# A list scheduler's costs: a sum that goes on in its PSUM tile, and four durations

## The chip, the cores and the metric

One core of a Trainium2 chip runs the whole program. The metric is device time in microseconds (us) of one execution, the median of three runs. The traces come from the hardware profiler and show one execution each.

## The reference, cut to what matters

Two decoder layers on x of shape (1, 512, 1024). Each layer normalizes x, projects it to 8776 columns with one weight matrix, and feeds three mixers whose outputs are gated, merged and multiplied with a last matrix:

```python
for l in range(DEPTH):                                  # DEPTH = 2
    h = rms_norm(x, norm_g[l])
    p = h @ w_in[l]
    (cb, cc, cx, cgate, q, k, v, agate, iq, ik, iw, pu, pgate, mgate) = split_columns(p)
    y_a = short_conv_mixer(cb, cc, cx, cgate, conv_w[l], w_out_conv[l])
    y_b = sparse_attention_mixer(q, k, v, agate, iq, ik, iw, ...)   # top 128 of up to 512 keys by an indexer's score
    y_c = pool_mixer(pu, pgate, pool_w[l], pool_scale[l], w_out_pool[l])
    g = jax.nn.sigmoid(mgate.reshape(B, S, N_BRANCHES, D))
    merged = g[:, :, 0] * y_a + g[:, :, 1] * y_b + g[:, :, 2] * y_c
    x = x + merged @ w_o[l]
```

## The kernel before, in words

Everything is kept transposed: 128 features on the partitions, the 512 positions along the free dimension. Every float32 operand of a matmul is split into a high and a low float32r part, and a product is the sum of three matmuls into one PSUM tile (`mm3`, line 393). A projection (`project`, line 456) takes one weight chunk of 128 x 1024 (`take`, line 375; `prep`, line 362, loads it, ACT makes the high part `whi` at line 371, DVE the low part `wlo` at line 372, three buffers of each) and adds up 8 x 3 matmuls of 512 columns in one of four PSUM tiles `pj`. DVE then reads the tile out (`evac`, line 385, or line 608, or line 819 at the end of a layer).

Beside the projections, TensorE computes scores in two tiles `sc`, and attention outputs in one tile `pv`, and transposes into one tile `pt`:

- `select` (line 556) makes the indexer's scores: per layer 24 pairs of matmuls of 256, 384 or 512 columns into an `sc` tile, each pair one sum (lines 563 and 564). Afterwards DVE finds the 128 largest of each row by 16 rounds of MAX8 and MATCH_REPLACE8 for each of three blocks of rows (lines 576 and 577).
- `attention` (line 712) runs twice in a layer over 16 blocks: a pair of matmuls of 128 to 512 columns into `sc` (lines 719 and 720), softmax on DVE and ACT (lines 724 to 730), one to four transposes into `pt` (line 738), which ACT and DVE split into a high and a low part (lines 741 and 742), and for each of 4 heads a sum of eight matmuls of 512, 512, 384, 384, 256, 256, 128 and 128 columns into `pv` (lines 748 to 753).

`merge` (line 591) multiplies a branch's output with its matrix, gates it, and adds it to the accumulators on GpSimd (line 610).

The order in which each engine issues is not the order of the code. The class `Order` (line 30) reads all instructions, gives each a cost (`cost`, line 108), and plays them through a model of the engines (`play`, line 139): whenever an engine is free, it takes that instruction among those ready that has the smallest priority number. For TensorE the number is the place in the program; for the others it is the time at which TensorE needs the result, worked out backwards from the pass before. An instruction is ready when what it depends on has ended, plus a latency from `LAT` or, for a reader on TensorE, from `TO_PE` (lines 37 and 38). Tiles with few buffers hold an instruction back until one is free. The play is repeated (`PASSES`, line 13), each time with new priorities, and the pass with the shortest modelled time is kept (`arrange`, line 247). It fixes each engine's order; on the chip an engine that reaches an instruction whose operands are not there waits, and all behind it with it.

With the latency of 0.003 from TensorE to TensorE, the next matmul of a sum is not yet ready at the moment at which the one before ends. So the play takes another sum's matmul, if one is ready, and two sums take turns in two PSUM tiles:

```python
LAT = {"PE": 0.2, "DVE": 0.13, "Activation": 0.14, "Pool": 0.1, "SP": 0.13}
TO_PE = {"PE": 0.003, "DVE": 0.255, "Activation": 0.27, "Pool": 0.2, "SP": 0.27}
    ...
ready[j] = max(ready[j], fin + self.lat(e, ops[j]["e"]))
```

Of the kernel before, what the change touches and what calls it, by code (L numbers as in the profile page):

```python
# [9 lines left out]
PSUM = bass.MemoryType.PSUM  # L10

LAG = 3
PASSES = 4
P = 128
S = 512
D = 1024
# [13 lines left out]
class Order:  # L30
# [4 lines left out]


    LAT = {"PE": 0.2, "DVE": 0.13, "Activation": 0.14, "Pool": 0.1, "SP": 0.13}
    TO_PE = {"PE": 0.003, "DVE": 0.255, "Activation": 0.27, "Pool": 0.2, "SP": 0.27}

    def lat(self, a, b):  # L40
        return self.TO_PE[a] if b == "PE" else self.LAT[a]

# [65 lines left out]
    def cost(self, inst, kind):  # L108

        def size(a):  # L110
            n = 1
            for _, k in a.bass_ap.ap[1:]:
                n *= k
            return n

        aps = [a for a in inst.ins if hasattr(a, "bass_ap")]
        out = inst.outs[0]
        n = size(out)
        psum = any(a.bass_ap.tensor.name.split("_")[0] in ("pj", "sc", "pt", "pv") for a in aps)
        wide = [a for a in aps if size(a) > 1]  # L120
        extra = len(aps) > len(wide)
        engine = str(inst.engine).split(".")[-1]
        if kind == "InstMatmult":
            f32 = str(aps[0].dtype).endswith("float32")
            c = (0.0004167 * n + 0.003) * ((4 if n > 128 else 2) if f32 else 1)
            return c, 0.0
        if kind == "InstDMACopy":
            b = n * out.bass_ap.ap[0][1] * 4
            return (0.65 if aps[0].bass_ap.tensor.name in self.slot else 0.48), b / 360e3
        if engine == "Activation":  # L130
            return 0.093 - 0.042 * psum + 0.000833 * n + 0.093 * extra, 0.0
        if engine == "Pool":
            return (0.1 if kind == "InstMemset" else 0.1 + 0.0022 * n), 0.0
        if kind in ("InstMax", "InstMatchReplace"):
            return 0.069 + 0.00104 * max(size(a) for a in aps), 0.0
        fast = kind == "InstTensorScalarPtr" and len(wide) == 1 and not psum
        return 0.069 + 0.00104 * n * (0.5 if fast else 1) + 0.061 * extra, 0.0

# [107 lines left out]

    def arrange(self, passes=PASSES):
        raw = self.read()
# [695 lines left out]
```

## Time and profile before

| | us |
|---|---|
| median of 3 runs (1078.87 to 1079.73) | 1079.21 |
| the profiled execution's own time | 1078.84 |
| its span, first to last instruction | 1077.1 |
| TensorE busy in it | 1065.4 |
| VectorE (DVE) busy | 799.2 |
| ScalarE (ACT) busy | 465.5 |
| GpSimd (POOL) busy | 97.2 |

The span lies inside the execution's own time; 1.7 us of that time lie around it. Matmuls are pipelined, so that the length of one in the trace (some 0.39 us for 512 columns) is longer than the distance from its start to the next one's start; the distance is what counts for the time. The granted TensorE clock of the span is 1.000 of full speed.

### The profile page before, as it was taken

The page shows a single profiled execution, that of the slowest core. Times are in us where ns is not written, and L with a number is a line of the kernel's source. Part 1 is how long each engine was busy: PE and PEld are TensorE (multiplying, and loading weights), DVE is VectorE, ACT ScalarE, POOL GpSimd, SP SyncE. Part 2 cuts the span into 40 slices and gives each one's busy share as a digit, 9 for nine tenths or more (in the row PEclk, how much of TensorE's full clock was granted, in tenths as well). Part 3 has the DMA queues.
Part 4 walks back from the last instruction along what each step waited for, and adds up shares of the span by engine and source line. Part 5 has one row for each costly group of instructions (what it writes and reads, how often), then busy time and mean ns, then how long its engine had stood idle before and what let it go on. Part 6 is the DMA issues. An engine that isn't in the chain of part 4 may idle for free.

```text
span 1077.1 us, 13444 instructions
## 1 busy us (share of the span) xinstructions
PE 1065.4 (99%) x4842; PEld 878.4 (82%) x4842; DVE 799.2 (74%) x1389; ACT 465.5 (43%) x747; POOL 97.2 (9%) x76
## 2 busy tenths in 40 slices
PE   7999999999999999999999999999999999999998
PEld 6888888888888888888888888888888878888886
DVE  6889999997558865455559899999876598744442
ACT  6355233485233673233334542235852347623320
POOL 4000000000000011221210000000000001132210
PEclk9999999999999999999999999999999999999999
DMA  6542322452234522234535322225423245122352
GB/s 226 153 140 78 99 98 94 133 152 72 82 102 130 160 75 78 98 98 164 169 117 153 115 86 98 98 79 166 128 79 98 79 144 149 61 98 98 98 195 78
DMA packets 44402, 124.39 MB, mean 115 GB/s; under 512 B 6960, under 2 KB 7472, under 8 KB 44336
## 3 DMA queue, kind: packets, MB, share of 16 engines
q1 hardware_dynamic: 44336, 123.53, 36.4%
q8 instruction: 38, 0.62, 0.2%
q14 instruction: 28, 0.23, 0.1%
HBM read 101.49 MB, written 4.19 MB: 98 GB/s over the span
## 4 chain that ended last, share of the span: by engine, by line
PE 96%; DVE 1%; DMA 1%; issue 0%; ACT 0%; SPq 0%; DVEq 0%; ACTq 0%
PE pj L388 87%; PE sc L388 4%; PE pv L388 3%; PE pt L391 2%; DMA b<-in_x 0%; DVE wlo L372 0%; DMA k<-h 0%; DVE w L488 0%; SPq L355 0%; DVE h L401 0%; ACT whi L371 0%; DVE w L649 0%; ACT xhi L403 0%; DVE w L435 0%; DVE w L436 0%
## 5 line engine op out<-in xcount | busy, mean ns | idle before, releaser
L388 PE MATMUL pj<-xhi,whi 128*128 128x512 f32 x1040 | 373.1, 393 | 6.5 <-ACT whi L371 6.5
L388 PE MATMUL pj<-xlo,whi 128*128 128x512 f32 x1040 | 372.8, 393 | 0.0
L388 PE MATMUL pj<-xhi,wlo 128*128 128x512 f32 x1040 | 372.4, 393 | 0.0
L371 ACT ACTIVATE whi<-raw 128x1024 fp32r<-128x1024 f32 (+2 forms) x185 | 191.5, 1036 | 385.6 <-PE pj L388 358.9
L372 DVE TENSOR_TENSOR wlo<-raw,whi 128x1024 fp32r<-128x1024 f32 (+2 forms) x185 | 228.5, 1239 | 15.5 <-ACT whi L371 14.8
L388 PEld LDWEIGHTS pj<-xhi,whi 128*128 128x128 f32 x1040 | 195.0, 188 | 46.7 <-ACT whi L371 6.7
L388 PEld LDWEIGHTS pj<-xhi,wlo 128*128 128x128 f32 x1040 | 195.7, 188 | 39.4 <-DVE wlo L372 0.5
L388 PEld LDWEIGHTS pj<-xlo,whi 128*128 128x128 f32 x1040 | 195.5, 188 | 39.4
L388 PE MATMUL pj<-b,whi 128*128 128x512 f32 x640 | 210.7, 390 | 0.0
L385 DVE TENSOR_TENSOR w<-pj,ss 128x512 f32<-128x512 f32 x104 | 70.8, 684 | 93.3 <-PE pj L388 93.0
L388 PEld LDWEIGHTS pj<-b,whi 128*128 128x128 f32 x640 | 120.0, 188 | 24.2
L388 PE MATMUL pj<-b,wlo 128*128 128x512 f32 x320 | 118.2, 391 | 0.0
L610 POOL TENSOR_TENSOR b<-b,w 128x512 f32<-128x512 f32 x32 | 60.6, 1899 | 264.5 <-DVE w L608 264.4
L388 PEld LDWEIGHTS pj<-b,wlo 128*128 128x128 f32 x320 | 60.1, 188 | 12.3
L576 DVE MAX8 m<-score 128x8 f32<-128x256 f32 (+2 forms) x96 | 53.2, 557 | 1.7
L577 DVE MATCH_REPLACE8 score<-m,score 128x384 f32<-128x384 f32 (+2 forms) x96 | 52.0, 542 | 0.0
L742 DVE TENSOR_TENSOR pth<-pt,pth 128x128 fp32r<-128x128 f32 (+1 forms) x64 | 31.1, 486 | 18.7 <-PE pv L388 9.4
L819 DVE TENSOR_TENSOR w<-pj,w 128x512 f32<-128x512 f32 x16 | 11.0, 690 | 44.4 <-PE pj L388 42.8
L727 ACT ACTIVATE a<-a,mn 128x128 f32<-128x128 f32 (+1 forms) x64 | 35.6, 557 | 15.5 <-DVE mn L724 14.9
L665 POOL TENSOR_TENSOR w<-w,w 128x512 f32<-128x512 f32 x8 | 11.9, 1492 | 325.4 <-ACT w L664 325.4
L388 PE MATMUL pv<-pth,b 128*128 128x512 f32 (+3 forms) x128 | 39.9, 316 | 0.0
L741 ACT ACTIVATE pth<-pt 128x128 fp32r<-128x128 f32 (+1 forms) x64 | 27.6, 432 | 27.4 <-PE pt L391 20.1
(119 smaller groups left out, 999.7 us busy)
## 6 DMA issues: line engine op xcount, KB each, us to landing
raw<-in_w SPq DMA_DIRECT2D x177, 512.0 KB, 3.3
b<-h SPq DMA_DIRECT2D x128, 64.0 KB, 2.2
k<-h SPq DMA_DIRECT2D x64, 128.0 KB, 3.2
b<-in_x SPq DMA_DIRECT2D x8, 256.0 KB, 4.8
w<-in_x SPq DMA_DIRECT2D x8, 256.0 KB, 5.5
xs<-w SPq DMA_DIRECT2D x8, 256.0 KB, 2.3
w<-xs SPq DMA_DIRECT2D x8, 256.0 KB, 3.9
out_x<-w SPq DMA_DIRECT2D x8, 256.0 KB, 2.0
```

The source lines that it names most:

```text
L371: act.activation(hi[:, p], raw[:, p], AF.Copy)
L372: dve.tensor_tensor(out=lo[:, p], in0=raw[:, p], in1=hi[:, p].bitcast(F32), op=ALU.subtract)
L385: dve.tensor_tensor(out=out, in0=ps, in1=by, op=ALU.mult)
L388: pe.matmul(ps, lhs, rhs, start=start, stop=stop)
L391: pe.transpose(out, src, ident if n == P else ident[64:64 + n, 64:64 + n])
L576: dve.max(m8, score)
L577: dve.match_replace(score, m8, score, -3.0e38)
L610: gp.tensor_tensor(out=a, in0=a, in1=g, op=ALU.add)
L665: gp.tensor_tensor(out=s0, in0=s0, in1=s1, op=ALU.add)
L727: act.activation(pr[:, :w], pr[:, :w], AF.Exp, bias=mn, scale=-1.0, accum_out=zs)
L741: act.activation(dh, pst[:, :b + 1, :], AF.Copy)
L742: dve.tensor_tensor(out=dl, in0=pst[:, :b + 1, :], in1=dh.bitcast(F32), op=ALU.subtract)
```

## The change

Six numbers of the scheduler change. No instruction is added or removed; only the order in which the engines issue can differ. The cost of a float32r matmul of n columns goes from 0.0004167 n + 0.003 to 0.000423 n + 0.01 (for 512 columns from 0.2163 to 0.2266), of a float32 transpose of 128 columns from 0.1127 to 0.1283, of a GpSimd operation on 512 elements from 1.226 to 1.636, of MATCH_REPLACE8 on 512 elements from 0.601 to 0.677. The latency between two matmuls goes to zero, and six passes are played in place of four.

```diff
-PASSES = 4
+PASSES = 6
...
-    TO_PE = {"PE": 0.003, "DVE": 0.255, "Activation": 0.27, "Pool": 0.2, "SP": 0.27}
+    TO_PE = {"PE": 0.0, "DVE": 0.255, "Activation": 0.27, "Pool": 0.2, "SP": 0.27}
...
-            c = (0.0004167 * n + 0.003) * ((4 if n > 128 else 2) if f32 else 1)
+            c = (0.000423 * n + 0.01) * ((4 if n > 128 else 2) if f32 else 1)
...
-            return (0.1 if kind == "InstMemset" else 0.1 + 0.0022 * n), 0.0
+            return (0.1 if kind == "InstMemset" else 0.1 + 0.003 * n), 0.0
         if kind in ("InstMax", "InstMatchReplace"):
-            return 0.069 + 0.00104 * max(size(a) for a in aps), 0.0
+            n = max(size(a) for a in aps)
+            return 0.069 + 0.00104 * n + 0.076 * (kind == "InstMatchReplace"), 0.0
```

## Rows read from the trace of the kernel before

**Rows 1.** The page: busy time of two engines, and the chain that ended last.

```profile
PE 1065.4 (99%) x4842; PEld 878.4 (82%) x4842; DVE 799.2 (74%) x1389; ACT 465.5 (43%) x747; POOL 97.2 (9%) x76
...
PE 96%; DVE 1%; DMA 1%; issue 0%; ACT 0%; SPq 0%; DVEq 0%; ACTq 0%
```

**Rows 2.** Waits of PE: who it waited for, us in total, times, longest us.

```profile
PE pj L388 <- ACT whi L371: 6.5, 1, 6.5
PE sc L388 <- DVE w L649: 0.6, 1, 0.6
PE sc L388 <- DVE w L401: 0.3, 1, 0.3
PE sc L388 <- DMA k<-h: 0.2, 1, 0.2
```

**Rows 3.** The chain that ended last, one piece: start us, us, what.

```profile
100.39 76.16 PE pj L388 x336
```

**Rows 4.** Timeline of PE inside that piece: start us, us, instruction.

```profile
101.13 0.39 PE L388 MATMUL pj<-xlo,whi 128*128 128x512 f32 x1
101.36 0.39 PE L388 MATMUL pj<-b,whi 128*128 128x512 f32 x1
101.58 0.39 PE L388 MATMUL pj<-xhi,wlo 128*128 128x512 f32 x1
```

**Rows 5.** Timeline of PE from 599.78 us, where one sum runs alone.

```profile
599.78 0.39 PE L388 MATMUL pj<-xhi,whi 128*128 128x512 f32 x1
600.01 0.39 PE L388 MATMUL pj<-xlo,whi 128*128 128x512 f32 x1
600.24 0.39 PE L388 MATMUL pj<-xhi,wlo 128*128 128x512 f32 x1
...
601.82 0.62 PE L388 MATMUL pj<-xhi,whi 128*128 128x512 f32 x2
```

**Rows 6.** Timeline of PE from 73.89 us: score pairs of `select`.

```profile
73.89 0.28 PE L388 MATMUL sc<-b,b 128*128 128x256 f32 x1
74.00 0.63 PE L388 MATMUL pj<-xhi,whi 128*128 128x512 f32 x2
74.47 0.28 PE L388 MATMUL sc<-b,b 128*128 128x256 f32 x1
74.58 0.40 PE L388 MATMUL pj<-xlo,whi 128*128 128x512 f32 x1
74.82 0.40 PE L388 MATMUL sc<-b,b 128*128 128x256 f32 x2
75.06 0.40 PE L388 MATMUL pj<-xhi,wlo 128*128 128x512 f32 x1
```

**Rows 7.** Timeline of PE from 235.46 us: the end of a sum in `pv`.

```profile
235.46 0.44 PE L388 MATMUL pj<-xhi,whi 128*128 128x512 f32 x1
235.74 0.22 PE L388 MATMUL pv<-pth,b 128*128 128x128 f32 x1
235.80 0.45 PE L388 MATMUL pj<-xlo,whi 128*128 128x512 f32 x1
```

**Rows 8.** Timeline of PE at its longest stop after the start.

```profile
604.37 0.40 PE L388 MATMUL pj<-xlo,whi 128*128 128x512 f32 x1
605.38 0.39 PE L388 MATMUL sc<-b,b 128*128 128x256 f32 x1 [0.61 <-DVE w L649]
```

**Rows 9.** Groups by line and shape: count, busy us, mean ns, idle before.

```profile
L372 DVE TENSOR_TENSOR wlo<-raw,whi 128x1024 fp32r<-128x1024 f32 x177 | 219.2, 1242 | 15.2 <-ACT whi L371 14.6
...
L610 POOL TENSOR_TENSOR b<-b,w 128x512 f32<-128x512 f32 x32 | 60.6, 1899 | 264.5 <-DVE w L608 264.4 <-POOL b L610 0.2
...
L577 DVE MATCH_REPLACE8 score<-m,score 128x512 f32<-128x512 f32 x32 | 21.6, 676 | 0.0
...
L742 DVE TENSOR_TENSOR pth<-pt,pth 128x512 fp32r<-128x512 f32 x16 | 11.0, 689 | 5.0 <-ACT pth L741 5.0
...
L741 ACT ACTIVATE pth<-pt 128x512 fp32r<-128x512 f32 x16 | 9.4, 590 | 6.8 <-PE pt L391 6.7
```

**Rows 10.** Windows: us, busy (x) of PE PEld DVE ACT POOL, clock, DMA share, GB/s.

```profile
100.00:180.00 80.00, 80.00 (x354) 66.25 (x353) 76.53 (x165) 25.11 (x29) 1.52 (x1) 1.00 0.30 99
180.00:220.00 40.00, 40.00 (x179) 32.78 (x178) 39.67 (x69) 18.63 (x27) 1.29 (x1) 1.00 0.49 138
```

**Rows 11.** Timeline at the end: the last read of PSUM.

```profile
1073.31 0.69 DVE L819 TENSOR_TENSOR w<-pj,w 128x512 f32<-128x512 f32 x1 [1.80 <-PE pj L388]
```

## The prediction

> **What bounds the kernel.** I read the page first. TensorE is busy 99% of the span and holds 96% of the chain that ended last; DVE is next with 74% [rows 1]. So I ask what TensorE does in the rest of the time, and whether its matmuls follow each other as closely as they can. The waits of TensorE answer the first: 6.5 us before the first matmul, and then three named waits that make 0.6 + 0.3 + 0.2 = 1.1 us [rows 2]. The chain's long piece answers the second: 336 matmuls in 76.16 us are 0.2267 us from one start to the next [rows 3]. A quiet stretch has nothing more to give, and the span from 6.5 us to the last read of PSUM at 1073.31 us [rows 11] is nearly all such stretches, plus the stretches of `select` and `attention`, in which short matmuls and transposes come in between.
>
> **What the change can reach.** It removes and adds no instruction, so the time can move in two ways only: by the price of a neighbourhood on TensorE (which matmul stands behind which), and by waits of TensorE that go or come because an order fits the chip's durations better or worse.
>
> **Part 1, the long sums.** Now two sums take turns: between the second and the third matmul of one product stands one of another sum [rows 4]. With the latency at zero the next matmul of a sum is ready when the one before it ends, has the smaller number, and is taken. What does a change of tile cost here? In the stretch with turns the distance is 0.2267 us [rows 3]; where one sum runs alone, nine distances from 599.78 to 601.82 make 2.04 us, or 0.2267 each [rows 5]. The same. Some 4,200 of the 4,842 matmuls are of this kind by the loops of the code, and I put them at **0 us**. The rows of the nine are rounded to 0.01 us, which leaves 0.001 us for each; if about half of the 4,200 take turns today, that is 2 us either way, and the range has to hold it.
>
> **Part 2, the score pairs.** There are 2 x 24 pairs in `select` and 4 x 16 in `attention`, 112 in all, 224 matmuls. Taking turns, an `sc` matmul of 256 columns and two long ones take 74.47 - 73.89 = 0.58 us, so the short one costs 0.58 - 0.453 = 0.127; the next one with one long matmul takes 74.82 - 74.47 = 0.35, so 0.123. Side by side, two of them behind a long one take 75.06 - 74.58 = 0.48, or 0.127 each [rows 6]. So standing side by side is worth nothing that these rows show; their rounding leaves 0.01 us for each matmul either way, 224 x 0.01 = 2.2 us. I take **0**, and keep -2.2 and +2.2 us.
>
> **Part 3, the sums in `pv`.** Sixteen sums of eight, 128 matmuls. Taking turns, a long matmul and one of 128 columns take 235.80 - 235.46 = 0.34 us, so the short one costs 0.115 [rows 7]. Before shows no two of 128 columns of one such sum side by side. From below: the columns alone, a quarter of 0.2267, are 0.057; with 32 such matmuls here and as many among the scores that is 64 x 0.058 = 3.7 us to gain. From above: the price of today and the rounding, +0.01 for each of 128, 1.3 us lost. The nearest row is that of the pair of 256 columns, whose price did not move, so I stay near today's price: **-0.5 us**.
>
> **Part 4, the durations.** The plan of before lets TensorE run at 0.2163 us for a long matmul, 4.6% faster than the chip does. The other engines were planned too fast as well: `wlo` at 0.069 + 0.00104 x 1024 = 1.134 us against 1.242, the read of transposed tiles at 0.601 against 0.689 on DVE and 0.478 against 0.590 on ACT, MATCH_REPLACE8 at 0.601 against 0.676, the GpSimd sum at 1.226 against 1.899 [rows 9]. So errors of the same sign partly cancelled. The change mends TensorE (0.2266), MATCH_REPLACE8 (0.677) and most of GpSimd (1.636), and leaves `wlo` and the reads as they are. GpSimd's 32 sums lie beside matmuls (its engine idles 264.5 us before them), so I put that edit at 0; if that cover went, 32 x 0.41 us of better foresight would be at stake. Two more passes can only find a plan that the model likes better. What is to be had is the waits: of the 1.1 us named and the stop at 604.37 us, where 1.01 us pass from one start to the next in place of 0.23 [rows 8], I take **-0.5 us**. All of them gone would be -1.1 us, with the unnamed rest of the stop -1.3; what new waits could cost stands with the second rival. The 6.5 us at the start hang on the first weights and stay; one ACT operation of 0.6 us moved past the first `whi` would be the bound either way. At the end nothing stands behind the last sum but one DVE read and its DMA, in either order.
>
> **The sum.** 0 + 0 - 0.5 - 0.5 = -1.0 us. Against the profiled execution's own time (1078.84, which is 1.7 above its span) that is 1077.8; the median of the runs shown is 0.37 us higher, so **1078.2 us**. A measurement of this kernel can tell some 0.2%, 2.2 us, from no change: the forecast counts as no change.
>
> **The rivals.**
>
> *Side by side is cheaper, and the waits go.* If every `sc` matmul gains the 0.01 us that the rounding hides (2.2 us), the `pv` sums 1.0 and the waits 1.1, the time is 1079.2 - 4.3 = 1074.9. For it: a sum done sooner frees `sc` and `pv` sooner, which the loops of `select` and `attention` wait for. Against: rows 6. Chance 0.22.
>
> *Short matmuls side by side overlap.* The whole 3.7 us of part 3 in place of 0.5 give 1078.2 - 3.2 = 1075.0. For it: 0.06 us pass from the `pv` matmul to the long one behind it, so the short one does not hold the next matmul for longer; against: the long one before it is held 0.28 us in place of 0.227 [rows 7], so the price is paid there. Chance 0.08. The Trainium skill (TensorE: Matmul & The Clock Gate, Back-to-back issue gap) gives some 81 ns for each matmul in a sustained stream of loads and matmuls of 128 columns; by it the 64 short ones would save an estimated 64 x 0.034 = 2.2 us, while the trace's own price, where each stands alone, is 115 ns, so the rule is open until two stand side by side.
>
> *Slower: the margin is gone.* The 4.6% by which TensorE was planned too fast put more matmuls into each gap than the plan said, and covered the other engines' too short costs. With TensorE right, ACT and DVE are 10 to 23% slower than planned (1.242 for 1.134, 0.590 for 0.478) before what waits on them. The place is the loop from transposes over the two reads of `pt` (one buffer) to the next transposes, 64 times, and the loop over the two `sc` tiles, 48 times in `select`. A loop of about 2 us loses 4.6% of cover, 0.1 us; if TensorE arrives early by that in all 112, 11 us are lost, in one of three 3.7 us. In one of three, the time is 1078.2 + 3.7 = 1081.9. It decides from the point at which DVE has no slack: it is busy 76.53 of 80 us and 39.67 of 40 us in the search for the largest scores [rows 10]. Against: TensorE is busy all of those stretches today, and the search itself is what the change plans better. Chance 0.17.
>
> *The change does not do what it says.* If a play with the old kind of turns remains the best, or the order differs where nothing waits, the time stays at 1079.2. Chance 0.08, inside no change.
>
> **How the numbers follow.** Forecast 0.45, rivals 0.22, 0.08, 0.17 and 0.08. Of the forecast's own chance some 0.06 falls below 1077.05, the bound of faster. So faster is 0.22 + 0.08 + 0.06 = 0.36, no change 0.39 + 0.08 = 0.47, slower 0.17. The range reaches down to the two faster rivals with a little room, 1074.5, and up to the lower part of the slower one, 1081.4. The likeliest case alone is 1077 to 1079.5.
>
> **What would show it.** In the changed kernel's timeline the two parts of a product should stand behind each other (`xhi,whi`, `xlo,whi`, `xhi,wlo`) at 0.227 us, score pairs should show as x2, and `pv` sums as runs of eight. A window of a long projection stretch should hold as many matmuls as before; if it holds more, part 1 is wrong. Two `pv` matmuls of 128 columns side by side give the missing price of part 3. In the waits of TensorE, more than 2 us behind the start, with ACT and DVE as those waited for, would be the slower rival; none at all the first.

## The result, and the profile after

The changed kernel takes 1087.20 us (median of 4 runs, 1085.29 to 1088.57) against 1079.04 (4 runs, 1078.71 to 1079.73) of the kernel before: a ratio of 1.0074, with an interval of 1.0056 to 1.0091. It is slower by 8.2 us, outside what the interval leaves for no change, and outside the predicted range.

The profiled execution took 1088.57 us, its span 1086.4. Its line numbers from 136 on are one higher than before. First the busy times and the chain that ended last on its page, beside [rows 1]:

```profile
PE 1069.9 (98%) x4842; PEld 874.5 (80%) x4842; DVE 804.6 (74%) x1389; ACT 460.2 (42%) x747; POOL 84.2 (8%) x76
...
PE 80%; DVE 9%; ACT 4%; DMA 3%; issue 3%; SPq 1%; ACTq 0%; DVEq 0%
```

TensorE still looks full (98%), but its share of the chain fell from 96 to 80%: the chain now leaves TensorE for DVE, ACT and DMAs in many places. Had I read the busy share alone, I should have seen nothing. The waits of TensorE (total us, times, longest us), beside [rows 2]:

```profile
PE pj L389 <- ACT whi L372: 5.8, 2, 5.1
PE sc L389 <- ACT h L401: 2.3, 2, 1.2
PE pj L389 <- DVE wlo L373: 0.9, 2, 0.5
PE sc L389 <- DMA k<-h: 0.6, 1, 0.6
PE pv L389 <- ACT pth L742: 0.5, 1, 0.5
PE sc L389 <- DVE w L402: 0.5, 1, 0.5
PE pt L392 <- DVE w L530: 0.4, 1, 0.4
PE pj L389 <- DVE w L487: 0.4, 1, 0.4
PE pt L392 <- DVE pth L743: 0.4, 2, 0.2
PE pj L389 <- DVE xlo L405: 0.3, 1, 0.3
```

The first line holds the start (5.1) and a new wait of 0.7; with the nine below it that is 7.0 us behind the start, in place of 1.1. From all start-to-start distances of the trace, counting what a distance holds beyond the usual pitch of its shape (its median) where that is over 0.12 us, I get 26 stops of together 12.4 us, in place of 10 of together 3.1. (The view counts the time in which TensorE stood idle, this list what the next start lost, so it is the longer; the 0.7 at the second weights are 1.18 in it. Left out of it, at the very start, until about 12 us before and 11 us after, are the distances of 0.427 us at which the long matmuls follow there: the lower level of the clock.) This sum, "stops" below, is 9.3 us more, of the 10.7 by which the time from the first matmul's start to the last one's grew (1066.4 to 1077.1). The first matmul came 1.4 us earlier, which gives part of it back.

Where it was lost shows in windows of TensorE alone (start:end, length, busy us with matmuls, granted clock, DMA share, GB/s), first of the kernel before, then of the one after:

```profile
6.50:100.00 93.50, 93.49 (x411) 1.00 0.47 147
100.00:220.00 120.00, 120.00 (x532) 1.00 0.36 112
540.00:640.00 100.00, 99.39 (x449) 1.00 0.38 117
640.00:760.00 120.00, 120.00 (x536) 1.00 0.38 120
```

```profile
6.50:100.00 93.50, 90.17 (x394) 1.00 0.45 145
100.00:220.00 120.00, 120.00 (x532) 1.00 0.38 115
540.00:640.00 100.00, 97.86 (x440) 1.00 0.36 112
640.00:760.00 120.00, 120.00 (x535) 1.00 0.38 119
```

Over the whole span the changed kernel is 43 matmuls behind at 1073 us, and 26 of them are lost at the heads of the two layers: 17 before 100 us and 9 from 540 to 640. The search for the largest scores, where DVE has no slack and where I had put the point from which the slower rival decides, loses none in the first layer (532 and 532) and one in the second. The granted clock is printed as 1.00, full speed, in all of them; only the first matmuls of the span, told above, follow at the lower level in both kernels. The head of a layer is where the projections feed short chains: TensorE to DVE or ACT, through an SP-issued move of 64 KB, into the next splits. The longest stop of the first layer after the start, in the timeline (TensorE, ACT, DVE, then SP's queue):

```profile
65.54 0.39 PE L389 MATMUL pj<-xlo,whi 128*128 128x512 f32 x1
66.94 0.50 PE L389 MATMUL sc<-h,whi 128*128 128x512 f32 x1 [1.01 <-ACT h L401]
...
66.26 0.63 ACT L401 ACTIVATE h<-w 128x512 fp32r<-128x512 f32 x1 [2.43 <-DMA b<-h]
...
66.92 0.69 DVE L402 TENSOR_TENSOR h<-w,h 128x512 fp32r<-128x512 f32 x1 [1.95 <-ACT h L401]
...
55.01 10.89 SPq L356 DMA_DIRECT2D b<-h  x15
```

From 65.54 to 66.94 are 1.40 us in place of 0.23. Read it backwards: the matmul wants `h`, ACT makes it at 66.26 after 2.43 us of waiting for a DMA that still reads the tile it must write into, and that DMA is one of 15 that SP issues in a row from 55.01 to 65.90. The plan has 0.65 us for each, and 14 of them follow at that in the mean; one takes 1.73 us to issue, and that one makes the row some 1.2 us late, about what TensorE loses (1.17). The kernel before has such a move at about the same time. The two moves, after and before, in SP's timeline:

```profile
57.53 1.73 SPq L356 DMA_DIRECT2D b<-h  x1
...
55.77 1.52 SPq L355 DMA_DIRECT2D b<-h  x1
```

Before, no stop of TensorE follows on it: the first matmul on `h` there starts at 69.70, 0.22 us behind its neighbour. In an engine with a fixed order all later matmuls, ready or not, stand behind one that waits. In the second layer the matmul on `h` starts 1.64 us behind its neighbour in place of 0.23; there the 16 moves keep the plan's pace, but begin late.

The neighbourhoods did change as foretold. Timeline of TensorE after: a sum that goes on in its tile, then pairs of `sc`, then a run of `pv`.

```profile
120.14 0.39 PE L389 MATMUL pj<-xlo,whi 128*128 128x512 f32 x1
120.36 0.39 PE L389 MATMUL pj<-xhi,wlo 128*128 128x512 f32 x1
120.59 0.39 PE L389 MATMUL pj<-xhi,whi 128*128 128x512 f32 x1
...
70.69 0.64 PE L389 MATMUL sc<-b,b 128*128 128x256 f32 x4
71.17 0.39 PE L389 MATMUL pj<-xlo,whi 128*128 128x512 f32 x1
...
260.51 1.15 PE L389 MATMUL pv<-pth,b 128*128 128x512 f32 x7
261.49 0.45 PE L389 MATMUL pj<-xhi,wlo 128*128 128x512 f32 x1
```

And one piece of its chain (start us, us, what), beside [rows 3]:

```profile
102.84 75.25 PE pj L389 x332
```

75.25 / 332 = 0.2267 us: the pitch of the long matmuls is that of before, to four digits. So the loss is not in the price of a long matmul; most of it (9.3 us of 10.7) is in stops.

### The profile page after: what moved, and what is told of

Same layout as the page of the kernel before. It is cut to its first block, busy times and chain, and to the rows that moved or that the text cites. A ratio compares the mean times of both kernels' runs of the same rounds, so it can differ in the third digit from the quotient of the medians.

```text
span 1086.4 us, 13426 instructions
## 1 busy us (share of the span) xinstructions
PE 1069.9 (98%) x4842; PEld 874.5 (80%) x4842; DVE 804.6 (74%) x1389; ACT 460.2 (42%) x747; POOL 84.2 (8%) x76
## 4 chain that ended last, share of the span: by engine, by line
PE 80%; DVE 9%; ACT 4%; DMA 3%; issue 3%; SPq 1%; ACTq 0%; DVEq 0%
PE pj L389 72%; PE sc L389 4%; PE pv L389 3%; DVE wlo L373 2%; PE pt L392 2%; DMA b<-h 1%; DMA raw<-in_w 1%; SPq L356 1%; ACT whi L372 1%; DVE h L402 1%; DVE w L489 1%; DVE w L487 1%; ACT a L728 0%; ACT xhi L404 0%; DVE w L491 0%
## 5 line engine op out<-in xcount | busy, mean ns | idle before, releaser
L389 PE MATMUL pj<-xhi,whi 128*128 128x512 f32 x1040 | 408.7, 393 | 6.2 <-ACT whi L372 5.8
L389 PE MATMUL pj<-xhi,wlo 128*128 128x512 f32 x1040 | 408.1, 393 | 0.9 <-DVE wlo L373 0.9
L389 PE MATMUL pj<-xlo,whi 128*128 128x512 f32 x1040 | 407.3, 392 | 0.3 <-DVE xlo L405 0.3
L373 DVE TENSOR_TENSOR wlo<-raw,whi 128x1024 fp32r<-128x1024 f32 (+2 forms) x185 | 238.2, 1290 | 28.7 <-ACT whi L372 27.9
L389 PE MATMUL pj<-b,whi 128*128 128x512 f32 x640 | 198.9, 390 | 0.0
L389 PE MATMUL pj<-b,wlo 128*128 128x512 f32 x320 | 125.0, 391 | 0.0
L611 POOL TENSOR_TENSOR b<-b,w 128x512 f32<-128x512 f32 x32 | 45.7, 1427 | 281.7 <-DVE w L609 281.7
L578 DVE MATCH_REPLACE8 score<-m,score 128x256 f32<-128x256 f32 (+2 forms) x96 | 52.0, 542 | 0.0
L609 DVE SCALAR_TENSOR_TENSOR w<-w,pj 128x512 f32<-128x512 f32 x32 | 21.9, 685 | 32.2 <-ACT b L404 16.8
L401 ACT ACTIVATE h<-w 128x512 fp32r<-128x512 f32 (+1 forms) x36 | 22.7, 630 | 51.8 <-DVE w L490 24.1
```

Of the source, the lines that this page charges most:

```text
L373: dve.tensor_tensor(out=lo[:, p], in0=raw[:, p], in1=hi[:, p].bitcast(F32), op=ALU.subtract)
L389: pe.matmul(ps, lhs, rhs, start=start, stop=stop)
L401: act.activation(hi, src, AF.Copy)
L578: dve.match_replace(score, m8, score, -3.0e38)
L609: dve.scalar_tensor_tensor(a if first else g, g, 1.0, py, op0=ALU.add, op1=ALU.mult)
L611: gp.tensor_tensor(out=a, in0=a, in1=g, op=ALU.add)
```

## The experiments

Every kernel below does the same work; only the orders differ. All were timed beside the kernel before, which had a median of 1079.0 to 1079.1 each time. Two theories lead. **Margin**: planning TensorE 4.6% too fast was a cover for all that the model leaves out (landing times, queues, buffers); at the true pace an operand is planned to arrive just in time, comes late, and TensorE stops. **Draw**: any edit of the costs deals another order, and orders scatter by some us, whatever the edit. **Turns** is the other half of the change: that sums no longer take turns.

### The halves apart

`e1`: the kernel before with the latency at zero. `e2`: the changed kernel with 0.003 again. `e3`: the changed kernel with the old matmul cost. `e4`: the changed kernel with 0.2 us more latency from every other engine to TensorE.

```diff
-    TO_PE = {"PE": 0.003, "DVE": 0.255, "Activation": 0.27, "Pool": 0.2, "SP": 0.27}
+    TO_PE = {"PE": 0.0, "DVE": 0.255, "Activation": 0.27, "Pool": 0.2, "SP": 0.27}     # e1; e2 the reverse
...
-            c = (0.000423 * n + 0.01) * ((4 if n > 128 else 2) if f32 else 1)
+            c = (0.0004167 * n + 0.003) * ((4 if n > 128 else 2) if f32 else 1)          # e3
...
+    TO_PE = {"PE": 0.0, "DVE": 0.455, "Activation": 0.47, "Pool": 0.4, "SP": 0.47}       # e4
```

> The kernel before with one edit: the latency from TensorE to TensorE is 0 in place of 0.003; all durations as before, so TensorE is still planned 4.6% too fast. Theory M (the margin went with the matmul's true duration): no loss, 1077 to 1081 us, waits of TensorE behind the start under 2.5 us. Theory T (two sums taking turns is itself what kept TensorE fed): as slow as the change, 1084 to 1090. Theory C (any new order is a draw, and the one of before was a lucky one): anywhere from 1077 to 1090.

> The changed kernel with the latency of 0.003 back, so that two sums take turns again; durations as changed. Theory M: still slow, 1083 to 1090, since TensorE is planned at its true pace. Theory T: back to 1077 to 1081. Theory C: anywhere from 1077 to 1090.

> The changed kernel with the matmul's old cost, 0.0004167 n + 0.003, so that TensorE is planned 4.6% too fast again; sums still go on in their tile. Theory M: back to 1077 to 1081. Theory T: still slow, 1084 to 1090. Theory C: anywhere.

> The changed kernel with 0.2 us more on each latency into TensorE (DVE 0.455, ACT 0.47, GpSimd 0.4, SP 0.47), so that a matmul is planned only when its operand is surely there; matmul cost true, sums go on in their tile. Theory M: the margin is back in another form, 1076 to 1082, waits of TensorE behind the start under 3 us. Theory T: no help, 1084 to 1090. Theory C: anywhere.

| kernel | us | ratio to before, interval | stops, us |
|---|---|---|---|
| e1, latency zero alone | 1082.86 | 1.0032 (1.0020 to 1.0044) | 5.7 |
| e2, after with turns | 1091.42 | 1.0113 (1.0097 to 1.0128) | 11.1 |
| e3, after with old matmul cost | 1080.71 | 1.0015 (1.0005 to 1.0024) | 6.1 |
| e4, after with wide latencies | 1086.85 | 1.0071 (1.0054 to 1.0088) | 10.4 |

The matmul cost carries most of it: taking it back alone (e3) gives back 6.5 of the 8.2 us. Bringing the turns back (e2) makes it worse by 4.2, so the turns half is not the cause. But e1, the turns half alone at the old pace, is 3.7 us slower than before, where margin had foreseen no loss: a draw, or the turns, or both. A wider latency in front of TensorE (e4) does not help, against what margin had foreseen (1076 to 1082): 0.2 us of fixed latency there is not the cover that went.

### The pace alone

The changed kernel with four other matmul costs, and the kernel before with one; 512 columns then take, as planned, 0.2215 (`e6`), 0.2368 (`e7`), 0.2105 (`e11`, and `e12` in the kernel before). The chip takes 0.2267. A fifth, `e5` (0.0004 n, 10% too fast, expected at 1076 to 1081), gives no time: its engines' orders deadlock.

```diff
-            c = (0.000423 * n + 0.01) * ((4 if n > 128 else 2) if f32 else 1)
+            c = (0.00042 * n + 0.0065) * ((4 if n > 128 else 2) if f32 else 1)           # e6
+            c = (0.000443 * n + 0.01) * ((4 if n > 128 else 2) if f32 else 1)            # e7
+            c = (0.00041 * n + 0.0006) * ((4 if n > 128 else 2) if f32 else 1)           # e11, e12
```

> The changed kernel with a matmul planned at 0.00042 n + 0.0065 (0.2215 us, 2.3% faster than the chip), half way between e3 and the change. Theory M: between them, 1082 to 1086. Theory C: no relation, 1077 to 1090.

> The changed kernel with a matmul planned at 0.000443 n + 0.01 (0.2368 us, 4.5% slower than the chip). Theory M: worse than the change, 1090 to 1098, with more stops of TensorE behind DVE and ACT. Theory C: no relation, 1077 to 1090.

> The changed kernel with a matmul planned at 0.00041 n + 0.0006 (0.2105 us, 7% faster than the chip). Theory M: the next point of the series 0.2368, 0.2266, 0.2215, 0.2163: no worse than 1080.7, 1077 to 1081; below it nothing is left to gain but single stops. Theory C: anywhere to 1090.

> The kernel before with the matmul planned at 0.00041 n + 0.0006 (7% too fast in place of 4.6%), all else as before, so sums take turns. Theory M: as fast as before or faster, 1075 to 1080. Theory C: 1077 to 1090.

| planned for 512 columns | kernel | us | ratio, interval | stops, us |
|---|---|---|---|---|
| 0.2105 (7% fast) | e11 | 1081.93 | 1.0023 (1.0013 to 1.0033) | 6.9 |
| 0.2105, with turns | e12 | 1088.11 | 1.0081 (1.0064 to 1.0099) | 10.9 |
| 0.2163 (4.6% fast) | e3 | 1080.71 | 1.0015 (1.0005 to 1.0024) | 6.1 |
| 0.2215 (2% fast) | e6 | 1083.35 | 1.0042 (1.0027 to 1.0056) | 6.1 |
| 0.2266 (true) | after | 1087.20 | 1.0074 (1.0056 to 1.0091) | 12.4 |
| 0.2368 (4.5% slow) | e7 | 1113.84 | 1.0323 (1.0307 to 1.0338) | 34.6 |

From 4.6% fast to 4.5% slow the time only rises, as the margin theory has it, though each row is one order, and the step from e3 to e6 (2.6 us, with stops alike) is no larger than the scatter between orders shown below. The price of 4.5% slow is more than margin had foreseen (1090 to 1098). Waits of TensorE in e7:

```profile
PE sc L389 <- ACT w L401: 6.7, 5, 2.2
PE pj L389 <- ACT whi L372: 5.6, 2, 5.1
PE sc L389 <- DVE mn L725: 4.4, 5, 2.0
PE sc L389 <- DMA k<-h: 2.8, 2, 1.5
```

The second line is the start. The others are of the kinds seen in the changed kernel (splits, the moved `k`, the small chains), and several times longer. A plan that thinks TensorE slow leaves the feeding work for later. Too much margin does not go on helping, which margin had not foreseen (e11 1077 to 1081, e12 1075 to 1080): e11 and e12 have a few long stops. Waits of TensorE in e12:

```profile
PE pj L388 <- DVE b L710: 2.4, 1, 2.4
PE pj L388 <- DVE w L486: 1.8, 1, 1.8
PE pt L391 <- DVE w L529: 1.3, 1, 1.3
```

In the first two TensorE stops for reads by DVE of tiles in PSUM that it wants to write again, in the third for an operand. These stops stand in the plan itself. Played again, the scheduler of e12 leaves TensorE idle for 2.79, 1.95 and 1.53 us in front of these three instructions, where the chip lost 2.55, 1.94 and 1.50; that of e11 plans 3.72 us in front of the one that loses 2.40. So at 7% the model itself can no longer feed its TensorE without stops. The changed kernel's plan has one stop of 0.64 us behind its start (0.58 on the chip); the other 22 that the chip shows behind 12 us are in no plan.

### Is it the number, or the draw?

Each cost was moved by a hair: the true one (`n1`: 0.0095, `n2`: 0.0105 in place of 0.01) and the old one, in the changed kernel (`n3`: 0.0025, `n4`: 0.0035 in place of 0.003).

> The changed kernel with a matmul planned 0.5 ns shorter (0.000423 n + 0.0095): another order, at the same pace. Theory M (the true pace is what costs): 1085 to 1090, as the change. Theory C (the order of the change was an unlucky draw): back towards 1080 to 1083.

> The changed kernel with a matmul planned 0.5 ns longer (0.000423 n + 0.0105). Theory M: 1085 to 1090. Theory C: back towards 1080 to 1083.

> The changed kernel with the old matmul cost less 0.5 ns (0.0004167 n + 0.0025), a neighbour of e3. Theory M: 1079 to 1083, as e3. Theory C: as far from e3 as the change is, up to 1088.

> The changed kernel with the old matmul cost plus 0.5 ns (0.0004167 n + 0.0035), the other neighbour of e3. Theory M: 1079 to 1083. Theory C: up to 1088.

| pace | kernels | us |
|---|---|---|
| true | after, n1, n2 | 1087.20, 1087.96, 1087.61 |
| 4.6% fast, no turns | e3, n3, n4 | 1080.71, 1075.95, 1077.23 |

The means are 1087.6 and 1078.0: 9.6 us lie between the paces, while the three orders of a pace scatter over 0.8 and 4.8 us. So the pace decides, and a draw is worth a few us at the old pace. All eight kernels at the old pace (before, e1, e3, n3, n4, and e10, n6 and n7 from further down) lie between 1075.95 and 1082.86, and the five at the true pace with the feeders' costs as changed (after, n1, n2, e2, e4) between 1086.85 and 1091.42. The row of moves shows the cover at work: in all eight of the first kind one move takes 1.09 to 1.97 us, and TensorE does not stop at the first matmul on `h`; in after, n1, n2 and e7 a move of 1.5 to 1.9 us stops it there for 1.17 to 1.33 us (e2 does not stop there, e4 for 0.26). `n3` (ratio 0.9972, interval 0.9960 to 0.9983) is faster than both kernels, by 3.1 us than before. Its chain and waits of TensorE:

```profile
PE 96%; issue 1%; ACT 1%; DVE 1%; DMA 0%; SPq 0%; DVEq 0%
...
PE pj L389 <- ACT whi L372: 6.4, 1, 6.4
PE sc L389 <- issue: 0.8, 2, 0.5
PE pj L389 <- DVE wlo L373: 0.7, 2, 0.4
```

TensorE again holds 96% of the chain, with 2.9 us of stops.

### Can the cover be put where it belongs?

If the margin is a ratio between TensorE and what feeds it, then the true matmul cost with slower planned feeders must do as well. `e8`: DVE and ACT costs times 1.048. `e9`: every DMA lands 1 us later. `n5`: both.

```diff
-            return 0.093 - 0.042 * psum + 0.000833 * n + 0.093 * extra, 0.0
+            return 1.048 * (0.093 - 0.042 * psum + 0.000833 * n + 0.093 * extra), 0.0    # e8, n5; the two DVE lines alike
...
-                        fin = dma + 0.78
+                        fin = dma + 1.78                                                 # e9, n5, n7
...
-                need[i] = (min(s) if s else t) - c - (x + 1.43 if x else 0)
+                need[i] = (min(s) if s else t) - c - (x + 2.43 if x else 0)              # e9, n5, n7
```

> The changed kernel, matmul cost true, with all costs of DVE and ACT times 1.048, so that the pace of TensorE against these two is the one of e3; DMA, GpSimd and the latencies as changed. Theory M, if the pace against DVE and ACT is what counts: 1078 to 1083. If it is the pace against DMA, GpSimd or the latencies: still 1085 to 1090.

> The changed kernel, matmul cost true, with every DMA planned to land 1 us later (in the play and in the priorities). Theory D (what comes late is the DMAs: the splits behind line 401 wait for the moves that read their buffers): 1079 to 1083 us, and the stops behind the splits of line 401 and behind k<-h go. Theory M (the pace of TensorE against DVE and ACT is what counts): 1085 to 1090.

> The changed kernel, matmul cost true, with DVE and ACT costs times 1.048 (as e8) and every DMA 1 us later (as e9). Theory M in the form that the margin counts against whatever feeds TensorE, not in the matmul's number itself: as good as the old pace, 1076 to 1082 us. If the number itself counts: 1083 to 1088.

| kernel | us | ratio, interval | stops, us |
|---|---|---|---|
| e8, DVE and ACT slower | 1083.32 | 1.0045 (1.0030 to 1.0060) | 9.3 |
| e9, DMAs later | 1085.54 | 1.0059 (1.0043 to 1.0076) | 9.7 |
| n5, both | 1078.73 | 0.9998 (0.9989 to 1.0008) | 3.8 |

With both, the true matmul cost gives the time of the kernel before. Waits of TensorE in n5:

```profile
PE pj L389 <- ACT whi L372: 6.4, 1, 6.4
PE pj L389 <- DVE wlo L373: 0.6, 2, 0.4
PE pt L392 <- DVE pth L743: 0.6, 2, 0.3
PE sc L389 <- DVE w L402: 0.3, 2, 0.2
```

The waits for `h` and `k` are gone. Either cover alone gives back less (3.9 and 1.7 us, both with an interval that overlaps that of the changed kernel, the first by a hair) than both together (8.5). So what counts is the margin against DVE, ACT and the DMAs, and not that the matmul's number is wrong. Each of the three is one order, so how the 8.5 us divide between the two covers is not shown.

### What turns, the other two costs and the DMAs are worth at the old pace

`e10` is the kernel before with the new costs of MATCH_REPLACE8 and GpSimd and six passes, so the changed kernel without its two TensorE edits. `n6` is n3 with the latency of 0.003, `n7` is n3 with the later DMAs.

> The kernel before with the new costs of MATCH_REPLACE8 and GpSimd and six passes alone; matmul cost and the latency of 0.003 as before. Theory M: TensorE is still planned 4.6% too fast, so no loss, 1076 to 1081. Theory C (each order is a draw): 1077 to 1090.

> n3 with the latency of 0.003 back, so that two sums take turns: the other half of the change by itself at the old pace. If going on in the tile helps at this pace as it did at the true one (the change against e2): 1079 to 1084. If it is worth nothing, as the prediction had it: 1075 to 1078.

> n3 with every DMA planned 1 us later, the only edit that cut the stops at the true pace by itself without the pace. If DMA landings still stop TensorE at the old pace: 1073 to 1076. If the pace covers them: 1075 to 1079.

| kernel | us | ratio, interval |
|---|---|---|
| e10 | 1082.67 | 1.0032 (1.0021 to 1.0043) |
| n6 | 1079.10 | 0.9999 (0.9990 to 1.0009) |
| n7 | 1078.01 | 0.9991 (0.9981 to 1.0000) |

Four pairs now differ by the turns alone: without them the time changes by -3.2 (n6 to n3), -2.0 (e10 to e3), -4.2 (e2 to after) and +3.7 (before to e1), -1.4 us in the mean. Every pair is also a draw, so this is a lean and no proof. n7 shows that the cover of n5 is not simply added: on top of the fast pace a later DMA buys nothing (2.1 us slower than n3).

The way from before to after can be walked in three steps: match, GpSimd and passes +3.6 (e10), then the latency -2.0 (e3), then the matmul cost +6.5: +8.1. The first step mends two costs that were too short and still loses, against what margin had foreseen for e10 (1076 to 1081); whether that is more than a draw is not shown. The six passes have no part in any of it: with four the planned order is the same on every engine, instruction by instruction, so the pass that is kept is among the first four.

## Why the prediction was wrong

**Part 1, the long sums (0 us): right.** 0.2267 us in both, as the chain's piece shows. The range had to hold 2 us either way; to four digits none of it was needed.

**Part 2, the score pairs (0): right.** Four matmuls of 256 columns side by side take 71.17 - 70.69 = 0.48 us, 0.12 each, against 0.123 to 0.127 [rows 6].

**Part 3, the `pv` sums (-0.5): right in kind, small.** Seven of a sum now stand together, the last two with 128 columns. Over the 16 such runs the median distances from the two short ones to the next start are 0.060 and 0.112 us, 0.086 each. Over the 32 places of the kernel before where one stood alone, a long matmul and a short one took 0.318, so the short one cost 0.091, and not the 0.115 that I took from a single place (its rows give 0.113 [rows 7]): 16 of the 32 take some 0.34 as that one does, and the other 16 some 0.29, which a view of all would have shown. The two short ones of a sum so save 0.01 us, 16 x 0.01 = 0.2 us in all. The rival of overlap is refuted with its 3.7 us. The Trainium skill (TensorE: Matmul & The Clock Gate, Back-to-back issue gap) gives some 81 ns for each matmul of this width in a sustained stream. The 86 ns measured for the pair come near it. Since a single one costs 91, there was nothing to save.

**Part 4, the durations (-0.5): the step that failed.** I argued that "the other engines were planned too fast as well", so that mending TensorE would leave a better plan, and took half of the waits as gone. The term of -0.5 measured +9.3: the stops grew by 9.3 us. Two errors made it. First, I compared planned costs with lengths of instructions. On DVE, as on TensorE, the length in the trace is more than the distance to the next one. Timeline of DVE after, where it has work without a gap:

```profile
52.13 0.67 DVE L487 TENSOR_TENSOR w<-pj,ct 128x512 f32<-128x512 f32 x1
52.73 1.20 DVE L373 TENSOR_TENSOR wlo<-raw,whi 128x1024 fp32r<-128x1024 f32 x1
53.86 0.67 DVE L402 TENSOR_TENSOR h<-w,h 128x512 fp32r<-128x512 f32 x1
```

The first takes 0.67 us by its length and 0.60 by its pitch, the second 1.20 and 1.13; the plan has 0.601 and 1.134. So these operations were planned right in the kernel before, and so was ACT's read of the transposed tiles (0.478 planned; 0.49 before and 0.48 after are the median distances where the next operation follows without a gap). They were not planned too fast, as TensorE was. I had told of exactly this difference for matmuls and did not use it for DVE and ACT. Second, I took a truer number for a better plan. The 4.6% was a margin, and the change took it out; what the model leaves out (the one move of 1.73 us at the stop shown above, for one) was then uncovered.

**The rival "the margin is gone": right that the excess pace was a cover, wrong in what it covered, in place, price and chance.** It said that it covered the too short costs of ACT and DVE, and gave a loss of 3.7 us, 1081.9 and 0.17; the loss is 8.2, and those costs were not too short. The places it named lost little: the stops before attention's `pt` make 1.5 us of the 12.4 and those before the score pairs of `select` none, and the search, where DVE is full, lost one matmul. Most went at the heads of the layers, the two longest behind the start in the chain through the moves. I looked for the point where an engine has no slack, but TensorE stopped where it waited for one late operand and no engine need be full. My price, one in three of 112 loops at 0.1 us, came from loops of which each would lose a little; the trace has 26 stops, six of which, of 0.67 to 1.41 us, make 5.9 of the 12.4.

**The two other rivals.** "Side by side is cheaper and the waits go" is refuted: the waits came. Its time (1074.9) is close to n3 (1075.95), which has the new neighbourhoods and the old pace; but its gain was to come from prices, and n3's stops (2.9 us) are about those of before (3.1). "The change does nothing" is refuted by the neighbourhoods.

**What stays open.** Which of the model's omissions makes a true-cost plan late, apart from the slow move at the one stop. Both covers together recover all, a fixed latency nothing; no run mended one omission (the slow moves, the late start of a row of moves) by itself. How far n3's 1075.95 is a better place and how far a lucky draw is open as well, since n4, a hair away, has 1077.23.

## What to carry to other kernels

An order fixed in advance is judged by how it bears what its model leaves out, so plan an engine that must never wait a little faster than it is (here 4.6%; the orders tried at 2% and at 7% were slower than e3 beside them), or its feeders a little slower, and do not call it an error to be mended before it is known what it covers. When costs are compared with a trace, compare pitches from start to start, over all instances. And since neighbouring numbers deal orders that differ by several us, judge a scheduler's change by a few neighbours of each setting, and keep the best order that was measured.

## What the hardware showed that I had not expected

A DVE operation's length in the trace overstates its price as a matmul's does: 0.67 against 0.60 us for 512 elements, 1.20 against 1.13 for 1024. GpSimd's sums of 512 elements fell from 1.899 us [rows 9] to a mean of 1.427 without any edit to them (32 of them, 45.7 us in all): the length goes with the turns. In the five kernels with turns (before, e2, e10, e12, n6) the mean is 1.63 to 1.90, in the fifteen others 1.29 to 1.43; why is not shown, and the profile's spans on GpSimd are rough.

In e7 one long stop costs more than its own length. Windows of TensorE there (columns as above), around the stop from 226.56 to 228.92 us:

```profile
226.00:228.00 2.00, 0.95 (x5) 1.00 1.06 293
228.00:232.00 4.00, 3.08 (x10) 0.66 0.46 154
232.00:236.00 4.00, 4.00 (x20) 0.92 0.00 0
```

Behind it the granted clock is 0.66 of full over four us, and long matmuls follow each other at 0.43 us (230.51 to 230.94 to 231.37) in place of 0.2267: the lower of the two levels, 1.2 GHz. Some seven matmuls lost 0.2 us each, 1.4 us on top of the 2.1 of the stop. Length alone does not decide it: no such matmuls follow on e7's own stop of 2.31 us at 729.83, or on one of 2.55 in e12 (219.91); seven follow in e12 on two stops close together (1.50 and 1.94, from 47.96). The changed kernel's stops, at most 1.41 us, show nothing of this.
